# A two-layer trunk on one core: the squares' rows of x, the first unit's eviction and the rotary tables moved to other slots

## The chip, the cores and the metric

The kernel runs on one core of a Trainium2 chip. The metric is the device time of one execution in microseconds (us), taken as the median of several runs. A profiled execution is recorded besides; its trace has a start and an end for each instruction, and its times are counted from the first instruction. "PE" is the matrix engine (TensorE), "ACT" the ScalarE, "DVE" the VectorE, "POOL" the GpSimd engine; SP is the queue that issues most loads.

## The reference

Two layers of one mixer, on 256 rows of 2048 values (float32). Cut to what matters here:

```python
def hybrid_layer(x, cos, sin, norm_g, w_in, conv_w, conv_b, ...):
    h = rmsnorm(x, norm_g)
    proj = h @ w_in                                    # 2048 x 13376
    (c_a, c_glu, c_gate, q_down, kv_down, k_pe, m_gate, g_conv, g_mla) = jnp.split(proj, idx, axis=-1)
    y_conv = conv_branch(c_a, c_glu, c_gate, conv_w, conv_b, ...) @ w_proj_conv
    y_mla = mla_branch(q_down, kv_down, k_pe, m_gate, cos, sin, ...) @ w_proj_mla
    y = jax.nn.sigmoid(g_conv) * y_conv + jax.nn.sigmoid(g_mla) * y_mla
    return x + y @ w_out

def conv_branch(a, glu, gate, conv_w, conv_b, ln_g, ln_b):
    u = a * jax.nn.sigmoid(glu)
    u = (causal depthwise convolution of u, 31 taps) + conv_b
    u = jax.nn.silu(layernorm(u, ln_g, ln_b))          # over the 2048 channels
    return u * jax.nn.silu(gate)

def rope_tables(positions, dtype):
    inv_freq = ROPE_THETA ** (-jnp.arange(0, QK_ROPE, 2, dtype=jnp.float32) / QK_ROPE)
    ang = positions.astype(jnp.float32)[..., None] * inv_freq
    return jnp.cos(ang), jnp.sin(ang)
```

`rmsnorm` divides each row of x by the root of the mean of its squares. The kernel multiplies `x * norm_g` with the weights at once and applies that factor (`rinv_x`) to the products, so that it is not needed before the first products are taken out of PSUM.

## The kernel before

**Pieces.** Every product runs over the weights in pieces of 256 rows (two blocks of 128) by 320, 384 or 512 columns, one DMA each, numbered here in the order of their use: 0 to 31 are the first block of units (`glu` 0, which is 512 wide, and the three `down` blocks of 384, 384 and 320, their first two pieces interleaved), 276 is the first piece of the convolution's projection `pconv` in the first layer. A piece is split into a rounded part `hi` and a remainder `lo`: ACT casts `hi` (`split_hi`), DVE subtracts (`split_lo`), and PE multiplies high by high, low by high and high by low, 12 matmuls a piece, eight with `hi` and then four with `lo`. The activations x * g are split in the same way, on the way in, for pieces 0, 4 and 8 to 13 (`first_h`, from `x_in`).

**Buffers.** There are five buffers of raw pieces, four of `hi` and three of `lo`. So the load of a piece waits until the piece five before it is split, the cast of `hi` until PE is through with the `hi` of four before, and `lo` until PE is through with the piece three before. Splits are issued three (`HI_AHEAD`) and two (`LO_AHEAD`) pieces ahead of PE's.

**Order.** `InOrder` keeps every engine in the order of the program text that issues: what stands in an engine's queue waits for all that stands ahead of it. After each piece, `background` advances the slot clock by one (slot k follows piece k - 1) and issues what is due: `at_slot(ahead, f, ...)` puts a function on a later slot, with the cost in us that it takes of the budgets of DVE and ACT. Whatever budget is left to DVE in a slot is spent on `fill`, a first-in-first-out list that holds the convolutions (31 taps for each of eight units), and behind them the layer norm: sums over channels (`mu`, `var`, two small matmuls each), its root, the scaled and gated channels `v_t`, and at last the split `ycT` of the convolution branch, which is what `pconv` multiplies. `before_pconv` runs what is left of that list when a piece of `pconv` needs it; so the place of `ycT` in ACT's order follows from how far `fill` has come.

**The start.** In the first layer the squares of x come from eight tiles `xres` (four pairs of 128 x 512, loaded by `first_sums(t, c)`'s `begin` on SP, squared on ACT by its `end` into `ss_x`). `sum_x` adds them on DVE (`totx`) and takes the root in thirteen small instructions (`rinv_x`). Behind it come the evictions: `glu_evac` (a sigmoid on ACT, a product `su` on DVE, then the turn through DRAM that brings channels to partitions and starts the first convolution) and `down_evac` (a scaled copy). The rotary tables are made by `rope_tables`, a generator whose twelve reductions and four last steps are 3 or 4 small DVE instructions each, one step to a slot.

The lines that order this, before:

```python
at_slot(8 + a + (2 if a < 2 else 7), lambda: next(tables, None), 0.0 if a < 2 else 0.95)   # a in range(20)
...
at = 7                                                         # eviction of the first glu unit
for n, (t, c) in enumerate([(0, 0), (0, 2), (1, 0), (1, 2)]):
    begin, end = first_sums(t, c)
    at_slot((11, 12, 13, 17)[n], begin)
    at_slot((15, 16, 17, 20)[n], end, 0.0, 1.5)
at_slot(20, sum_x, 2.2)
```

Of the kernel before, what the change touches and what calls it, by code (L numbers as in the profile page):

```python
# [11 lines left out]
F32 = mybir.dt.float32  # L12
# [7 lines left out]
P = 128  # L20
T = 2
# [9 lines left out]
HALF = ROPE // 2  # L31
# [53 lines left out]
def revolution_pieces():  # L85

    from fractions import Fraction

    pi = Fraction(
        "3.14159265358979323846264338327950288419716939937510582097494459230781640628620899"  # L90
    )
    rest, out = 1 / (2 * pi), []
    for i in range(REVOLUTION_PIECES):
        unit = Fraction(1, 1 << (12 * (i + 1)))
        n = int(rest / unit)
        out.append(float(n * unit))
        rest -= n * unit
    return out
# [33 lines left out]
def trunk(ctx: ExitStack, tc: tile.TileContext, xT, x, g_in, pos, win, wuq, wukv, wpc, wpm, wo, cst, rows, invf, out):  # L132
# [19 lines left out]
    pe, vec, act, gps, sp = (InOrder(e) for e in (nc.tensor, nc.vector, nc.scalar, nc.gpsimd, nc.sync))  # L152
# [7 lines left out]
    work = pool("work", 1)  # L160
    work2 = pool("work2", 2)
# [147 lines left out]
    def at_slot(ahead, f, vec=0.0, act=0.0, first=False):  # L309
        steps.insert(0 if first else len(steps), (clock[0] + ahead, (vec, act), f))  # L310
# [280 lines left out]
    def rope_tables():  # L591

        invf_t = const.tile([P, HALF], F32, name="invf_t")
        sp.dma_start(invf_t, invf.partition_broadcast(P))
        pos_t = const.tile([P, T], I32, name="pos_t")
        sp.dma_start(pos_t, pos)
        yield
        yield
        posf = const.tile([P, T], F32, name="posf")
        vec.tensor_copy(posf, pos_t)  # L600
        tables = work.tile([P, 6, T, HALF], F32, tag="pr", name="tables")
        ang, ah, al, turn, whole, frac = (tables[:, i] for i in range(6))
        ah = ah.bitcast(F32R)
        for t in range(T):
            vec.tensor_scalar(ang[:, t, :], invf_t, posf[:, t : t + 1], None, op0=ALU.mult)
        vec.tensor_copy(ah, ang)
        vec.tensor_sub(al, ang, ah.bitcast(F32))
        yield
        big_half = 1.5 * 2.0**23

        def reduce_to(dst, src, scale):

            vec.tensor_scalar(whole, src, scale, big_half, op0=ALU.mult, op1=ALU.add)
            vec.tensor_scalar(whole, whole, -big_half, None, op0=ALU.add)
            vec.scalar_tensor_tensor(dst, src, scale, whole, op0=ALU.mult, op1=ALU.subtract)

        first = True
        for piece in revolution_pieces():
            for a in (ah.bitcast(F32), al):
                reduce_to(turn if first else frac, a, piece)  # L620
                if not first:
                    vec.tensor_add(turn, turn, frac)
                first = False
                yield
        for dst, shift in ((sin2, 0.0), (cos2, 0.25)):
            vec.tensor_scalar(frac, turn, shift, None, op0=ALU.add)
            reduce_to(ang, frac, 1.0)
            for h in range(2):
                act.activation(dst[:, :, h, :], ang, AF.Sin, scale=2.0 * np.pi)
            yield  # L630
            yield
# [24 lines left out]
    def first_sums(t, c):  # L656

        xts = []

        def begin():  # L660
            for a in (c, c + 1):
                xts.append(wide_p.tile([P, 512], F32, tag="w", name="xres"))
                sp.dma_start(xts[-1], x[t, :, a * 512 : (a + 1) * 512])

        def end():
            for a, xt in zip((c, c + 1), xts):
                junk = work.tile([P, 512], F32, tag="junk", name="junk")
                act.activation(junk, xt, AF.Square, accum_out=ss_x[:, t, a : a + 1])

        return begin, end  # L670


    for l in range(DEPTH):
# [776 lines left out]

        def rope_table_steps():
            tables = rope_tables()
            for a in range(20):
                at_slot(8 + a + (2 if a < 2 else 7), lambda: next(tables, None), 0.0 if a < 2 else 0.95)

        uses_h = stat_of(h_hi, h_lo)
        of_down = lambda k0: lambda k, t: tuple(qkc[:, i, k0 + k, t * P : (t + 1) * P] for i in range(2))
        for kind, i, pl in planned:
            if kind == "glu":
                at = 0 if i in (2, 5) else EVAC_AT  # L1460
                if i == 0 and l == 0:
                    at = 7
                    for n, (t, c) in enumerate([(0, 0), (0, 2), (1, 0), (1, 2)]):
                        begin, end = first_sums(t, c)
                        at_slot((11, 12, 13, 17)[n], begin)
                        at_slot((15, 16, 17, 20)[n], end, 0.0, 1.5)
                    at_slot(20, sum_x, 2.2)
                elif i == 0:
                    at_slot(8, sum_x, 2.2)
                if i == 0:  # L1470
                    for slot, load_const in zip(((22, 26), (4, 7))[l], load_consts):
                        at_slot(slot, load_const)
                if i == 0:
                    if l == 0:
                        rope_table_steps()
                    downs = FIRST_DOWNS[l]
                    products_together(
                        pl, uses_h, lambda i, t, ps: down_evac(i - 1, t, ps) if i else glu_evac(0, t, ps),
                        (at,) + downs * (EVAC_AT,), ((0.9, 2.2),) + downs * ((0.0, 1.0),),
                        homes=("acc", "acc") if l else ("s", "acc", "acc", "tp"),  # L1480
                    )
                    if downs == len(DOWN_BLOCKS):
                        down_after()
                    continue
                product(pl, uses_h, lambda t, ps, i=i: glu_evac(i, t, ps), at, (0.9, 2.2))
            elif kind == "down":
                product(pl, uses_h, lambda t, ps, i=i: down_evac(i, t, ps), costs=(0.0, 1.0))
                if i == len(DOWN_BLOCKS) - 1:
                    down_after()
            elif kind == "uq":  # L1490
                if i == 0:
                    attention_tiles()
                group, block = divmod(i, 3)
                product(pl, of_down(0), lambda t, ps, i=i: uq_evac(i, t, ps), costs=(0.0, (2.9, 2.7, 1.7)[block]))
                at_slot(EVAC_AT + 1, lambda b=GROUP * group + block: rotate_q(b), 1.3)
                if block == 2:
                    at_slot(EVAC_AT + LAST_ROTATE_AT, lambda b=GROUP * group + 3: rotate_q(b), 1.3)
                    attention(GROUP * group + 2)
            elif kind == "ukv":
                product(pl, of_down(4), lambda t, ps, i=i: ukv_evac(i, t, ps), costs=(0.36 * (i % GROUP == 2), 2.6))  # L1500
                if i % GROUP != 2:
                    attention(i)
                if i == NPAIR - 1:
                    layernorm()
            elif kind == "mgate":
                product(pl, uses_h, lambda t, ps, i=i: mgate_evac(i, t, ps), costs=(0.0, 3.5))
            elif kind == "gmla":
                product(pl, uses_h, lambda t, ps, i=i: gmla_evac(i, t, ps), costs=(0.0, 2.7))
            elif kind == "pmla":
                product(pl, stat_of(*keep["o"]), lambda t, ps, i=i: pmla_evac(i, t, ps), costs=(1.25, 0.0))  # L1510
            elif kind == "gconv":
                product(pl, uses_h, lambda t, ps, i=i: gconv_evac(i, t, ps), costs=(0.0, 3.9))
            elif kind == "cgate":
                product(pl, uses_h, lambda t, ps, i=i: cgate_evac(i, t, ps), costs=(0.0, 2.0))
            elif kind == "pconv":
                while "yc" not in keep:
                    run_fill()
                products_together(pl, stat_of(*keep["yc"]), pconv_evac, (EVAC_AT, EVAC_AT, EVAC_AT, 0), (2.4, 0.0), before_pconv, ("acc", "s", "tp", "acc"))
            elif i == 0:
                wout_begin(0)  # L1520
                wout_begin(1)
                products_together(pl, stat_of(*keep["y"]), wout_evac, (EVAC_AT, EVAC_AT), (1.25, 1.5))
            else:
                at_slot(3, lambda i=i: wout_begin(i))
                product(pl, stat_of(*keep["y"]), lambda t, ps, i=i, f=wout_evac: f(i, t, ps),
                        0 if i == 3 else EVAC_AT, (1.25, 1.5),
                        final=last_half if last_layer and i == 3 else None)
# [116 lines left out]
```

## Time and profile before

| what | value |
|---|---|
| median of 3 runs | 1791.65 us (1790.62 to 1792.54) |
| the profiled execution, its own time | 1791.25 us |
| its span, first to last instruction | 1789.5 us |
| granted clock of PE over the span | 0.999 |
| DMA traffic | 464.18 MB, mean 259 GB/s |

The page gives the busy time of each engine and the chain of work that ended last, of which PE makes 98%. Where PE is that full, its own waits say more than the chain: the view of waits names the engine and the tile that PE waited for, how long and how often; the timeline shows the rows around such a wait, with the idle time before a row and its releaser in brackets; and the windows give, for a stretch of time, the busy time of each engine and, in the third column from the right, the granted clock. A timeline row is a run of equal instructions, with its start, its length and their count.

### The profile page before, as it was taken

The numbers are of one execution on the slowest core, as the hardware profiler recorded it, in microseconds if no ns is written. First come the engines' busy times: TensorE is split into PE (matmuls) and PEld (weight loads), VectorE is DVE, ScalarE is ACT, GpSimd is POOL, SyncE is SP. The second block draws the span as 40 slices with busy tenths as digits, with TensorE's granted clock in tenths as the row PEclk, the third lists the DMA queues.
The fourth block names the chain that finished last, engine by engine and source line by source line (L and its number), as shares of the span: only waits on it lengthen the run. The fifth ranks groups of instructions, "written<-read, shape, count | busy, mean of one in ns | idle before, by whom it ended". The sixth has DMA issues, their size and how long they took to land.

```text
span 1789.5 us, 27098 instructions
## 1 busy us (share of the span) xinstructions
PE 1780.2 (99%) x8575; PEld 1573.0 (88%) x8575; DVE 1535.4 (86%) x2481; ACT 1297.3 (72%) x2404; POOL 553.7 (31%) x1015
## 2 busy tenths in 40 slices
PE   9999999999999999999999999999999999999999
PEld 8888888888888888888899888888888888888887
DVE  6799899898999998767668998988999999887674
ACT  6678888888877775745567788898888777666442
POOL 0155555542311120012420555656333111100210
PEclk9999999999999999999999999999999999999999
DMA  8788888887999996678887888888879889867785
GB/s 299 257 283 258 275 278 257 277 289 241 281 256 251 263 253 234 200 226 302 295 280 225 278 275 265 267 277 270 286 245 277 249 253 256 254 213 221 248 281 178
DMA packets 149967, 464.18 MB, mean 259 GB/s; under 512 B 24896, under 2 KB 31296, under 8 KB 149824
## 3 DMA queue, kind: packets, MB, share of 16 engines
q1 hardware_dynamic: 105568, 358.68, 61.7%
q0 software_dynamic: 43664, 103.24, 20.5%
q8 instruction: 67, 1.10, 0.3%
q14 instruction: 76, 0.62, 0.1%
q10 hardware_dynamic: 592, 0.54, 0.1%
HBM read 399.18 MB, written 44.04 MB: 248 GB/s over the span
## 4 chain that ended last, share of the span: by engine, by line
PE 98%; DMA 1%; ACT 0%; DVE 0%; issue 0%; SPq 0%; DVEq 0%; ACTq 0%
PE acc L143 95%; PE s L143 2%; PE o_ps L143 1%; DMA xres<-in_x 0%; DMA raw<-in_win 0%; ACT hi L143 0%; SPq L143 0%; ACT L143 0%; DVE rsq_t L143 0%; ACT v_t L143 0%; DVE xres L143 0%; ACT junk L143 0%; DVE lo L143 0%; DVE rinv_x L143 0%; ACT down L143 0%
## 5 line engine op out<-in xcount | busy, mean ns | idle before, releaser
L143 ACT CAST hi<-raw 128x1024 fp32r<-128x1024 f32 (+3 forms) x682 | 693.9, 1027 | 371.6 <-PE acc L143 277.8
L143 DVE TENSOR_TENSOR lo<-raw,hi 128x1024 fp32r<-128x1024 f32 (+3 forms) x682 | 811.9, 1194 | 154.9 <-PE acc L143 108.5
L143 PE MATMUL acc<-hi,hT 128*128 128x512 f32 (+2 forms) x1728 | 400.7, 372 | 0.0
L143 PEld LDWEIGHTS acc<-hi,hT 128*128 128x128 f32 x1728 | 319.7, 189 | 40.4
L143 PE MATMUL acc<-hi,h_hi 128*128 128x512 f32 (+2 forms) x864 | 251.2, 373 | 0.5 <-ACT hi L143 0.4
L143 PE MATMUL acc<-hi,h_lo 128*128 128x512 f32 (+2 forms) x864 | 250.7, 372 | 0.0
L143 DVE SCALAR_TENSOR_TENSOR v_t<-u_t,cst,v_t 128x256 f32<-128x256 f32 x556 | 237.3, 480 | 2.0
L143 PE MATMUL acc<-lo,h_hi 128*128 128x512 f32 (+2 forms) x864 | 220.5, 372 | 1.5 <-DVE lo L143 1.5
L143 PE MATMUL acc<-lo,hT 128*128 128x512 f32 (+2 forms) x864 | 220.2, 372 | 0.0
L143 PEld LDWEIGHTS acc<-lo,h_hi 128*128 128x128 f32 x864 | 160.7, 189 | 22.9 <-DVE lo L143 2.3
L143 PEld LDWEIGHTS acc<-hi,h_lo 128*128 128x128 f32 x864 | 161.5, 189 | 20.6
L143 PEld LDWEIGHTS acc<-lo,hT 128*128 128x128 f32 x864 | 160.8, 189 | 20.6
L143 PEld LDWEIGHTS acc<-hi,h_hi 128*128 128x128 f32 x864 | 160.3, 189 | 21.2 <-ACT hi L143 1.1
L143 POOL DMA_DIRECT2D turn_d<-gate x176 | 96.2, 554 | 218.7 <-DVE gate L143 157.9
L143 POOL DMA_DIRECT2D taps<-taps x73 | 64.2, 879 | 306.2 <-ACT taps L143 232.3
L143 ACT ACTIVATE taps<-u_t,cst 128x256 f32<-128x256 f32 x302 | 132.8, 498 | 0.3 <-DVE v_t L143 0.3
L143 PE MATMUL acc<-hi,ycT 128*128 128x512 f32 x512 | 124.0, 383 | 2.3 <-ACT ycT L143 2.2
L143 PE MATMUL acc<-hi,oT 128*128 128x512 f32 x512 | 122.2, 379 | 0.0
L143 PE MATMUL acc<-hi,yT 128*128 128x512 f32 x512 | 122.0, 378 | 0.0
L143 POOL DMA_DIRECT2D turned<-turn_d x88 | 50.2, 578 | 213.8 <-ACT hi L143 61.0
L143 PEld LDWEIGHTS acc<-hi,ycT 128*128 128x128 f32 x512 | 97.4, 191 | 17.0 <-ACT ycT L143 2.6
L143 PE MATMUL acc<-hi,qkc 128*128 128x512 f32 x448 | 110.4, 379 | 0.0
(181 smaller groups left out, 2356.8 us busy)
## 6 DMA issues: line engine op xcount, KB each, us to landing
raw<-in_win SPq DMA_DIRECT2D x384, 512.0 KB, 4.8
raw<-in_wpm SPq DMA_DIRECT2D x64, 512.0 KB, 4.9
raw<-in_wpc SPq DMA_DIRECT2D x64, 512.0 KB, 4.2
raw<-in_wo SPq DMA_DIRECT2D x64, 512.0 KB, 5.2
taps<-taps POOLq DMA_DIRECT2D x73, 256.0 KB, 6.1
raw<-in_wukv SPq DMA_DIRECT2D x32, 512.0 KB, 4.4
turned<-turn_d POOLq DMA_DIRECT2D x56, 256.0 KB, 5.5
raw<-in_wuq SPq DMA_DIRECT2D x24, 512.0 KB, 4.8
```

The source lines that it names most:

```text
L143: ins = getattr(self.engine, name)(*a, **k)
```

## The change

```diff
     def rope_tables():
         invf_t = const.tile([P, HALF], F32, name="invf_t")
-        sp.dma_start(invf_t, invf.partition_broadcast(P))
+        gps.dma_start(invf_t, invf.partition_broadcast(P))
         pos_t = const.tile([P, T], I32, name="pos_t")
-        sp.dma_start(pos_t, pos)
+        gps.dma_start(pos_t, pos)
...
-        tables = work.tile([P, 6, T, HALF], F32, tag="pr", name="tables")
-        ang, ah, al, turn, whole, frac = (tables[:, i] for i in range(6))
+        tables = work.tile([P, 4, T, HALF], F32, tag="sx", name="tables")
+        steps_of = work2.tile([P, 2, T, HALF], F32, tag="qr", name="table_steps", bufs=3)
+        ang, ah, al, turn = (tables[:, i] for i in range(4))
+        whole, frac = (steps_of[:, i] for i in range(2))
...
         def rope_table_steps():
             tables = rope_tables()
-            for a in range(20):
-                at_slot(8 + a + (2 if a < 2 else 7), lambda: next(tables, None), 0.0 if a < 2 else 0.95)
+            next(tables)
+            next(tables)
+            for slot in (5, 6, 7, 8, 15, 16, 17, *range(21, 32)):
+                at_slot(slot, lambda: next(tables, None), 0.95)
...
                 if i == 0 and l == 0:
-                    at = 7
+                    at = 5
                     for n, (t, c) in enumerate([(0, 0), (0, 2), (1, 0), (1, 2)]):
                         begin, end = first_sums(t, c)
-                        at_slot((11, 12, 13, 17)[n], begin)
-                        at_slot((15, 16, 17, 20)[n], end, 0.0, 1.5)
-                    at_slot(20, sum_x, 2.2)
+                        at_slot((9, 10, 11, 14)[n], begin)
+                        at_slot((13, 13, 14, 17)[n], end, 0.0, 1.5)
+                    at_slot(18, sum_x, 2.2)
```

The rows of x are asked for two slots sooner (the last pair three), squared two to three sooner, and the root is taken at slot 18 in place of 20. The first unit is evicted at slot 19 in place of 21. The two small loads for the tables go from SP, between weight loads, to POOL at the program's start. The tables no longer share a buffer with the gains, which are in use until x is split, so their steps can begin at slot 5; four come there, three at slots 15 to 17, none at 18 to 20, the rest from 21 on.

On SP's queue, before, the last pair of `xres` stands behind the load of piece 23 (a number behind `raw` is the piece's):

```order
L143 DMA xres_467<-in_x 128x512
L143 DMA xres_469<-in_x 128x512
L143 DMA raw20_475<-in_win 128x768
L143 DMA raw21_493<-in_win 128x768
L143 DMA raw22_515<-in_win 128x768
L143 DMA raw23_537<-in_win 128x768
L143 DMA xres_555<-in_x 128x512
L143 DMA xres_557<-in_x 128x512
```

and now, with the first pairs higher up too, behind that of piece 20:

```order
L143 DMA xres_450<-in_x 128x512
L143 DMA xres_452<-in_x 128x512
L143 DMA raw18_458<-in_win 128x768
L143 DMA raw19_476<-in_win 128x768
L143 DMA raw20_502<-in_win 128x768
L143 DMA xres_520<-in_x 128x512
L143 DMA xres_522<-in_x 128x512
L143 DMA raw21_528<-in_win 128x768
```

Each of the first three pairs moved past two weight loads, the fourth past three.

On DVE, before, the root (from `totx` to the last `rinv_x`; ten of its rows left out) stands behind `lo` of piece 21, and table steps stand on both sides of `lo` of piece 22:

```order
L143 TENSOR_TENSOR lo21_609<-raw21_493,hi21_589 128x768
L143 TENSOR_REDUCE totx_631<-ss_x_143 128x2
...
L143 SCALAR_TENSOR_TENSOR rinv_x_142<-rsq_t_635,rinv_x_142 128x2
L143 TENSOR_SCALAR tables_561<-tables_561 128x64 x2
L143 SCALAR_TENSOR_TENSOR tables_561<-tables_561 128x64
L143 TENSOR_TENSOR tables_561<-tables_561 128x64
L143 TENSOR_TENSOR lo22_651<-raw22_515,hi22_611 128x768
```

and now behind `lo` of piece 19, with no table step before `lo` of piece 23:

```order
L143 TENSOR_TENSOR lo19_594<-raw19_476,hi19_570 128x768
L143 TENSOR_REDUCE totx_612<-ss_x_143 128x2
...
L143 SCALAR_TENSOR_TENSOR rinv_x_142<-rsq_t_616,rinv_x_142 128x2
L143 TENSOR_TENSOR lo20_628<-raw20_502,hi20_596 128x768
L143 SCALAR_TENSOR_TENSOR su_646<-acc0_00_161,rinv_x_142,su_646 128x256
L143 SCALAR_TENSOR_TENSOR su_650<-acc0_01_162,rinv_x_142,su_650 128x256
L143 TENSOR_TENSOR lo21_664<-raw21_528,hi21_630 128x768
L143 TENSOR_TENSOR lo22_682<-raw22_550,hi22_666 128x768
```

The root moved up by two pieces, the first unit's `su` by two, and the table steps out from among them.

On ACT, much later, where `pconv` begins with piece 276, before (the number behind `v_t` tells one unit of the convolution from another):

```order
L143 CAST hi277_7766<-raw277_7678 128x1024
L143 ACTIVATE v_t_2615<-v_t_2615,cst_146 128x256 x2
L143 ACTIVATE v_t_4849<-v_t_4849,cst_146 128x256 x2
L143 CAST hi278_7788<-raw278_7703 128x1024
L143 CAST hi279_7824<-raw279_7724 128x1024
L143 ACTIVATE v_t_5479<-v_t_5479,cst_146 128x256 x2
L143 CAST ycT0_7809<-v_t_1035 128x512
L143 CAST ycT0_7809<-v_t_2615 128x512
L143 ACT_TABLE_LOAD
```

and now:

```order
L143 CAST hi276_7752<-raw276_7667 128x1024
L143 CAST hi277_7781<-raw277_7688 128x1024
L143 ACTIVATE v_t_5440<-v_t_5440,cst_146 128x256 x2
L143 CAST ycT0_7773<-v_t_970 128x512
L143 CAST ycT0_7773<-v_t_2138 128x512
L143 CAST hi278_7805<-raw278_7710 128x1024
L143 CAST hi279_7832<-raw279_7732 128x1024
L143 ACT_TABLE_LOAD
L143 ACTIVATE sc_7303<-acc268_0_7634,rinv_x_142 128x512
```

No line of the diff speaks of this place. Since the first unit is evicted sooner, its convolution enters `fill` sooner, and with the budgets that rule there the whole list has moved up by two pieces; the casts of `ycT` went past those of pieces 278 and 279.

## The prediction

> **What bounds the kernel now.** I read the page's busy shares first, then the waits of TensorE, then TensorE's rows at each wait, then the rows of the engine waited for. First the page:
>
> ```profile
> PE 1780.2 (99%) x8575; PEld 1573.0 (88%) x8575; DVE 1535.4 (86%) x2481; ACT 1297.3 (72%) x2404; POOL 553.7 (31%) x1015
> ```
>
> PE is busy 1780.2 us of a span of 1789.5 us. No reordering of other engines can bring more than the 9.3 us in which PE idles, and what PE loses while it is busy but slow. The waits of PE say where it idles:
>
> ```profile
> PE acc L143 <- ACT ycT L143: 2.2, 1, 2.2
> PE acc L143 <- DVE lo L143: 1.5, 2, 0.8
> ```
>
> Both are places in the first layer; what PE idles beside them is at its start and after its end. The timeline of PE at the place of the `lo` waits (each piece of weights is five rows: four of `hi`, one of `lo`; the first row of a piece is `hi,h_hi`):
>
> ```profile
> 51.18 0.49 PE L143 MATMUL acc<-hi,h_hi 128*128 128x384 f32 x2
> ...
> 53.13 0.49 PE L143 MATMUL acc<-hi,h_hi 128*128 128x384 f32 x2
> ...
> 56.12 0.49 PE L143 MATMUL acc<-hi,h_hi 128*128 128x384 f32 x2
> ...
> 59.03 0.49 PE L143 MATMUL acc<-hi,h_hi 128*128 128x384 f32 x2
> ```
>
> These are pieces 21 (51.18), 22 (53.13), 23 (56.12) and 24 (59.03). An undisturbed piece takes 53.13 - 51.18 = 1.95 us. Pieces 22 and 23 take 5.90 us from 53.13 to 59.03, where two take 3.90: **2.00 us are lost here**. A piece wants its `lo` after 8 of its 12 matmuls, 1.30 us after its start: piece 20 (started 49.23, 1.95 before 51.18) at 50.53, piece 21 at 52.48, piece 22 at 54.43.
>
> Why `lo` is late, in the rows of the SP queue, of ACT and of DVE:
>
> ```profile
> 37.15 5.85 SPq L143 DMA_DIRECT2D raw<-in_win  x4
> 43.05 0.90 SPq L143 DMA_DIRECT2D xres<-in_x  x2
> ```
> ```profile
> 49.53 0.63 ACT L143 ACTIVATE junk<-xres 128x512 f32<-128x512 f32 x1 [0.78 <-DMA xres<-in_x]
> ```
> ```profile
> 51.04 0.16 DVE L143 TENSOR_REDUCE totx<-ss_x 128x2 f32<-128x8 f32 x1 [2.30 <-ACT junk L143]
> ...
> 53.50 0.42 DVE L143 TENSOR_SCALAR tables<-tables 128x64 f32<-128x64 f32 x2
> ...
> 54.36 0.95 DVE L143 TENSOR_TENSOR lo<-raw,hi 128x768 fp32r<-128x768 f32 x1
> ...
> 56.48 0.88 DVE L143 SCALAR_TENSOR_TENSOR su<-acc,rinv_x,su 128x256 f32<-128x256 f32 x2 [0.32 <-ACT su L143]
> 57.27 0.95 DVE L143 TENSOR_TENSOR lo<-raw,hi 128x768 fp32r<-128x768 f32 x1
> ```
>
> The last pair of `xres` tiles is issued at 43.05 behind four weight loads and lands 6.5 us later, at 49.53. ACT squares it, DVE waits 2.30 us in its queue for the sum, and behind the root and one table step stands `lo` of piece 22 (54.36); behind another table step and the two `su` stands `lo` of piece 23 (57.27).
>
> The second place, the start of the convolution's projection (piece 276), again PE, then ACT:
>
> ```profile
> 728.17 0.59 PE L143 MATMUL acc<-lo,h_hi 128*128 128x512 f32 x2
> 731.02 3.65 PE L143 MATMUL acc<-hi,ycT 128*128 128x512 f32 x8 [2.25 <-ACT ycT L143]
> ...
> 735.59 1.89 PE L143 MATMUL acc<-hi,ycT 128*128 128x512 f32 x8
> ...
> 738.18 1.89 PE L143 MATMUL acc<-hi,ycT 128*128 128x512 f32 x8
> ```
> ```profile
> 723.53 1.03 ACT L143 CAST hi<-raw 128x1024 fp32r<-128x1024 f32 x1
> ...
> 728.42 1.05 ACT L143 CAST hi<-raw 128x1024 fp32r<-128x1024 f32 x1 [0.94 <-ACT hi L143]
> 729.37 1.09 ACT L143 ACTIVATE v_t<-v_t,cst 128x256 f32<-128x256 f32 x2
> 730.36 1.12 ACT L143 CAST ycT<-v_t 128x512 fp32r<-128x512 f32 x2
> 731.50 1.28 ACT L143 ACT_TABLE_LOAD   x1
> 732.80 1.27 ACT L143 ACTIVATE sc<-acc,rinv_x 128x512 f32<-128x512 f32 x2
> ```
>
> A piece of 512 columns takes 738.18 - 735.59 = 2.59 us, 0.216 a matmul. The two matmuls of the row at 728.17 would let piece 276 start at 728.60 and piece 277 at 731.19; it starts at 735.59. **4.40 us are lost here**, of which only 731.02 - 728.60 = 2.42 are waiting. The other 1.98 is PE at half speed; a window of 1 us shows the granted clock (0.50, the figure ahead of the last two):
>
> ```profile
> 732.00:733.00 1.00, 1.00 (x3) 0.82 (x4) 0.29 (x1) 0.99 (x2) 0.00 (x0) 0.50 0.72 184
> ```
>
> The wait itself: the cast of `ycT` stands in ACT's queue behind the cast of piece 279 (728.42), whose buffer, one of four, is that of piece 275, the last that PE multiplies before. So `ycT` cannot come before PE has run dry.
>
> The Trainium skill ("TensorE: Matmul & The Clock Gate", "What's actually happening") puts the fall to half clock behind an idle window of about 3.4 us. By that rule a gap of 2.42 us would cost nothing more, this place would be worth 2.42, and the sum below would come to 1787.2. The row above shows clock 0.50 behind the shorter gap, so for this execution the measurement decides.
>
> **The change part by part.**
>
> *Rows of x.* The four pairs are asked for at slots 9, 10, 11, 14 in place of 11, 12, 13, 17. The last pair before was the one at 43.05, slot 17; slot 14 is in the middle of the weight loads that begin at 37.15, so I take 37.5, and with the same 6.5 us it lands at 44.0 in place of 49.53. The two squarings that this pair needs last 1.5 us (49.53 to 51.04). The root (from 51.04 to the table step at 53.50, some 2.5 us) now stands right behind `lo` of piece 19, whose buffer, one of three, PE frees with piece 16 at 43.38 (51.18 - 4 x 1.95), so that this `lo` ends near 44.4. The root runs from 45.5 to 48.0. Then `lo` 20 ends at 49.0 (wanted 50.53: 1.5 to spare), the two `su` at 49.9 (the table load ahead of their sigmoid, 1.28 us, no longer follows `down` but runs while ACT waits for the root), `lo` 21 at 50.8 (wanted 52.48: 1.7 to spare), `lo` 22 at 51.8 (wanted 54.43). **Minus 2.00.** Bounds: the spare is used up if the pair lands 1.5 us later than I take; a landing after 49.53 would cost more than before.
>
> *Table steps.* A step is some 0.9 us (53.50 to 54.36), and none now stands between `lo` 19 and `lo` 22. Their number is the same. Four go to slots 5 to 8, where DVE is not the bound:
>
> ```profile
> 24.32 0.91 ACT L143 ACTIVATE h_hi<-x_in,gx 128x256 fp32r<-128x256 f32 x2 [1.34 <-DMA x_in<-in_xT]
> 25.13 1.03 ACT L143 CAST hi<-raw 128x1024 fp32r<-128x1024 f32 x1
> ```
> ```profile
> 27.17 0.59 PE L143 MATMUL acc<-hi,h_hi 128*128 128x512 f32 x2
> ```
>
> Here ACT waits for `x_in`, and piece 10 is split at 26.16 for PE at 27.17: 1.0 us to spare, the tightest of the pieces there. Four steps are some 3.5 us; each falls mostly into a wait of DVE for ACT. What is left delays a `lo` by up to half a us, and through the freed buffer the next load of SP. Between 0 and 3.5 - 1.0 = 2.5 us of PE; I take 0, since the waits for `x_in` come once per piece and the steps do too.
>
> *Two small loads from SP to POOL; other tags for the tables.* POOL has nothing else to issue before the first `su`, and `sx` and `qr` are not needed again before attention. I take 0. The two loads, 17 KB, now run beside the first weights, so PE could start later; as the end of the range I take 0.6, a tenth of the 6.5 us that a pair of `xres` thirty times their size takes to land.
>
> *First unit two slots sooner.* The convolution is a queue of steps taken as DVE's budget allows, so everything behind moves up: mean and variance stand two pieces sooner in PE's order, and at piece 276 the cast of `ycT` now stands behind `hi` 277, not 279. That cast's buffer is that of piece 273 and was free before 723.53. The last that `ycT` needs of DVE is this row, two pieces or 5.18 us sooner:
>
> ```profile
> 728.02 1.43 DVE L143 TENSOR_TENSOR v_t<-turned,v_t 128x256 f32<-128x256 f32 x4
> ```
>
> DVE is through at 729.45 - 5.18 = 724.3; ACT, with `hi` 277 at 724.6, `v_t` 1.09 and `ycT` 1.12, at 726.8 or before. PE wants it at 728.60: 1.8 to spare. No wait, so no half clock: **minus 4.40.** Late next would be `hi` 280: from 728.3 ACT now has `hi` 279 (1.05), a table load, two `sc` (1.3), a table load, four `v_t` (2.1) and `hi` 280 (1.05), in all 8.1 us, to 736.4; PE wants it at 728.60 + 4 x 2.59 = 738.96. Six fewer tap products on ACT and six more on DVE fall where PE does not wait at all; I take 0.
>
> *Sum.* The profiled run took 1791.25 us (span 1789.5 and 1.75 around it): 1791.25 - 2.00 - 4.40 = 1784.85. The median of the runs is 0.40 higher, so 1785.25; I give **1785.2**, 0.36% faster. No-change, about what a measurement can tell, is 0.2% or 3.6 us.
>
> **The rivals.**
>
> *The second place stays* (12%). Another operand of piece 276, or `hi` 280, is late, PE waits over 2 us there and the clock falls again. For it: three engines meet there and my spare is 1.8. Against: the order frees `ycT` from the end of the block. Only 2.00 is gained: 1789.6.
>
> *The change does not do what it says* (8%): the rows of x are asked for sooner but land no sooner, since `x_in` and weights fill the DMA engines. The root then ends at 53.5 as before, but now `lo` 20 waits behind it, ready at 54.5 and wanted at 50.53: 4.0 us of waiting and 2.0 at half clock, as at the second place. 1791.65 - 4.40 - 2.00 + 6.0 = 1791.2. Against it: an earlier load does not wait behind later ones in a queue.
>
> *A part of it* (8%): `lo` 20 or 21 still late by 1 to 2.5 us, 1786.2 to 1787.7; or the timed runs of before did not have the half clock that the profiled one had, so that only 2.42 can go at the second place: 1791.65 - 2.00 - 2.42 = 1787.2. For the latter: the three runs spread by 1.9 us, which is the size of that loss.
>
> *Slower* (4%): four squarings (3 us) now stand in ACT's queue ahead of `hi` 16, which PE wants at 49.23 - 4 x 1.95 = 41.43. If the first two pairs land at X, `hi` 16 is ready at X + 3.0 + 0.8, so PE waits from X = 37.6 on; the first pair is now issued behind the last `x_in`, the second one piece later:
>
> ```profile
> 27.82 0.43 SPq L143 DMA_DIRECT2D x_in<-in_xT  x1
> ```
>
> That is 28.3 and 30.9, and 6.5 later is 37.4. Every us more is one of PE, and a wait over 2 us costs 2.0 more by the clock. From X = 42 on the gain is gone; at X = 46 the time is 1791.65 - 6.4 + 8.4 + 2.0 = 1795.7. Against it: that is twice the time to landing of any such load before.
>
> **How the numbers follow.** Forecast 68%, its own range 1783.6 to 1786.2 (the runs before spread by that much and the small terms add to it). Faster by over 0.2% is under 1788.1: forecast and part, 0.76; same: the second place and the loads that land no sooner, 0.20; slower 0.04. The range must leave out no more than 2 in 10: with the part and the second place, up to 1789.6, it holds some 0.85 (a little of the forecast lies outside).
>
> **What would show it.** PE waits neither for `lo` nor for `ycT`; the windows behind 726 us show clock 1.00; the last `xres` pair is issued near 37.5 and squared before 46; the `totx` row follows `lo` of piece 19 with under 1.5 us of idle. The forecast is wrong if PE waits for `hi` between 25 and 43 us, or for `lo` at pieces 20 and 21, or shows clock 0.50 anywhere after its start.

## The result, and the profile after

The change makes the kernel faster by 0.24%: the ratio of the mean times is 0.9976, with a 95% interval of 0.9969 to 0.9984. The medians are 1786.33 us (16 runs) and, before, 1791.38 us (16 runs), 5.05 us apart. Ratios below are made in the same way, each against runs of the kernel before that were taken beside it. The profiled run took 1786.36 us. In it PE is busy for all but 6.7 us of the span. The page's first lines, of after:

```profile
span 1784.6 us, 27089 instructions
...
PE 1777.9 (100%) x8575; PEld 1575.3 (88%) x8575; DVE 1538.4 (86%) x2487; ACT 1295.4 (73%) x2398; POOL 551.7 (31%) x1014
```

The waits of PE, of after (engine and tiles waited for, then us in total, how often, the longest):

```profile
PE acc L143 <- ACT hi L143: 1.3, 2, 0.8
PE warm L143 <- PEq L1637: 0.8, 1, 0.8
```

The waits for `lo` and for `ycT` are gone. For `hi` there are two, both in pieces 0 and 1, where before had one of 0.4 us, ahead of piece 2. The first place, the timeline of PE, of after, first rows of pieces 21 to 24:

```profile
52.85 0.49 PE L143 MATMUL acc<-hi,h_hi 128*128 128x384 f32 x2
...
54.80 0.49 PE L143 MATMUL acc<-hi,h_hi 128*128 128x384 f32 x2
...
56.75 0.49 PE L143 MATMUL acc<-hi,h_hi 128*128 128x384 f32 x2
...
58.70 0.49 PE L143 MATMUL acc<-hi,h_hi 128*128 128x384 f32 x2
```

Pieces 22 and 23 take 58.70 - 54.80 = 3.90 us, where before they took 5.90. What stands behind it, in the rows of SP, of ACT and of DVE, of after:

```profile
39.32 1.16 SPq L143 DMA_DIRECT2D xres<-in_x  x2
```
```profile
47.03 0.63 ACT L143 ACTIVATE junk<-xres 128x512 f32<-128x512 f32 x1 [1.25 <-DMA xres<-in_x]
```
```profile
47.79 0.16 DVE L143 TENSOR_REDUCE totx<-ss_x 128x2 f32<-128x8 f32 x1 [0.55 <-ACT junk L143]
...
50.27 0.96 DVE L143 TENSOR_TENSOR lo<-raw,hi 128x768 fp32r<-128x768 f32 x1
51.14 0.87 DVE L143 SCALAR_TENSOR_TENSOR su<-acc,rinv_x,su 128x256 f32<-128x256 f32 x2
51.93 1.82 DVE L143 TENSOR_TENSOR lo<-raw,hi 128x768 fp32r<-128x768 f32 x2
```

The last pair of `xres` is issued at 39.32; its first tile lands at 45.0 (ACT squares it at 45.06) and its second at 47.0. DVE waits 0.55 us for the sum, where it waited 2.30. `lo` of piece 20 (50.27) is done at 51.23 and wanted at 52.20, so 0.97 us is left.

The second place, PE and then ACT, of after:

```profile
727.57 0.59 PE L143 MATMUL acc<-lo,h_hi 128*128 128x512 f32 x2
728.00 1.89 PE L143 MATMUL acc<-hi,ycT 128*128 128x512 f32 x8
...
730.60 1.89 PE L143 MATMUL acc<-hi,ycT 128*128 128x512 f32 x8
```
```profile
722.21 1.06 ACT L143 CAST hi<-raw 128x1024 fp32r<-128x1024 f32 x1 [0.51 <-ACT hi L143]
723.17 1.09 ACT L143 ACTIVATE v_t<-v_t,cst 128x256 f32<-128x256 f32 x2
724.16 1.12 ACT L143 CAST ycT<-v_t 128x512 fp32r<-128x512 f32 x2
725.19 1.04 ACT L143 CAST hi<-raw 128x1024 fp32r<-128x1024 f32 x1
```

`ycT` is cast behind `hi` of piece 277 (722.21) and is done 2.7 us before PE wants it. Piece 276 follows without a gap and takes 2.59 us, from 728.00 to 730.60: all of the 4.40 us is gone. (A piece's length is the difference of the starts of two first rows, taken before they are rounded, so that it can differ by 0.01 us from the rows shown.)

These two make 6.40 us; the profiled run is 4.89 faster. What was given back is at the start. ACT's casts of the first pieces, of before and then of after:

```profile
5.50 0.44 ACT L143 CAST hi<-raw 128x320 fp32r<-128x320 f32 x1
6.31 0.51 ACT L143 CAST hi<-raw 128x384 fp32r<-128x384 f32 x1 [0.36 <-DMA raw<-in_win]
8.13 1.82 ACT L143 CAST hi<-raw 128x1024 fp32r<-128x1024 f32 x2 [1.31 <-DMA raw<-in_win]
```
```profile
6.86 0.46 ACT L143 CAST hi<-raw 128x320 fp32r<-128x320 f32 x1 [1.34 <-DMA raw<-in_win]
...
8.18 0.51 ACT L143 CAST hi<-raw 128x384 fp32r<-128x384 f32 x1 [0.87 <-DMA raw<-in_win]
...
9.47 1.82 ACT L143 CAST hi<-raw 128x1024 fp32r<-128x1024 f32 x2 [0.77 <-DMA raw<-in_win]
```

The same casts stand 1.3 to 1.9 us later, each behind its weights' DMA. PE starts piece 2 at 10.56 us in place of 9.23: **1.33 us lost**. (Counted from PE's first product, which came 0.25 us sooner, at 4.56 in place of 4.81, it is 1.58; the expectations below take 1.6.) The page's windows of 1 us, of before and then of after, end with the DMA engines' share and the GB/s:

```profile
4.00:5.00 1.00, 0.90 (x5) 0.67 (x5) 0.96 (x3) 0.46 (x2) 0.00 (x0) 1.00 1.18 313
5.00:6.00 1.00, 1.00 (x7) 0.84 (x7) 0.90 (x3) 0.94 (x3) 0.00 (x0) 1.00 0.95 360
```
```profile
4.00:5.00 1.00, 0.90 (x6) 0.56 (x5) 0.96 (x3) 0.61 (x2) 0.00 (x0) 1.00 1.30 158
5.00:6.00 1.00, 0.91 (x6) 0.84 (x6) 1.00 (x3) 0.51 (x2) 0.00 (x0) 1.00 0.66 96
```

From 4 to 6 us the DMA engines move 158 and 96 GB/s where they moved 313 and 360. That is when the two small loads are under way, which POOL now issues at the start (the DMA issues in the first 9 us, of after: KB, and us from issue to landing):

```profile
invf_t<-in_invf POOLq DMA_DIRECT2D x1, 16.0 KB, 5.1
pos_t<-in_pos POOLq DMA_DIRECT2D x1, 1.0 KB, 5.0
```

The rest is small: pieces 11 and 12 took 0.33 us more (PE waits for `hi` of piece 12, behind the last `x_in`), piece 76 took 0.07 more, pieces 31 and 33 took 0.34 less. With -6.40 and +1.33 that makes -5.01 of the -4.89.

### The profile page after: what moved, and what is told of

It reads as the page before. It is cut to its first block, busy times and chain, and to the rows that moved or that the text cites. A ratio compares the mean times of both kernels' runs of the same rounds, so it can differ in the third digit from the quotient of the medians.

```text
span 1784.6 us, 27089 instructions
## 1 busy us (share of the span) xinstructions
PE 1777.9 (100%) x8575; PEld 1575.3 (88%) x8575; DVE 1538.4 (86%) x2487; ACT 1295.4 (73%) x2398; POOL 551.7 (31%) x1014
## 4 chain that ended last, share of the span: by engine, by line
PE 98%; DMA 1%; DVE 0%; ACT 0%; SPq 0%; issue 0%; DVEq 0%
PE acc L143 95%; PE s L143 2%; PE o_ps L143 1%; DMA x_in<-in_xT 1%; DMA raw<-in_win 0%; DVE lo L143 0%; SPq L143 0%; ACT hi L143 0%; DVE xres L143 0%; ACT h_hi L143 0%; DVE h_lo L143 0%; DVE table_steps L143 0%; PE var L143 0%; PE mu L143 0%; DVE tables L143 0%
## 5 line engine op out<-in xcount | busy, mean ns | idle before, releaser
L143 ACT ACTIVATE taps<-u_t,cst 128x256 f32<-128x256 f32 x292 | 128.4, 498 | 0.4 <-DMA taps<-taps 0.4
L143 PEld LDWEIGHTS acc<-hi,oT 128*128 128x128 f32 x512 | 97.0, 190 | 13.5
```

What stands on the lines that cost most here:

```text
L143: ins = getattr(self.engine, name)(*a, **k)
```

## The experiments

Three theories stood after this reading. **Steps**: the convolution's list moved up because the table steps end at slot 31 and no longer at 34; each takes 0.95 us of DVE's budget, and the line `budget[e] = min(budget[e], 0.0) + slot - split_us` lets no unused budget pass from one slot to the next, so a step at slots 5 to 8 takes nothing from the list and one at 34 does. **Unit**: the list moved up because the first unit is evicted sooner, as the prediction has it. **Small loads**: they cost the start its 1.33 us; against it stood scatter of the first loads. The runs below compute all that the reference asks for.

**Small loads late.** Both on SP in place of POOL, behind the first weights.

```
-        gps.dma_start(invf_t, ...)
+        sp.dma_start(invf_t, ...)
-        gps.dma_start(pos_t, pos)
+        sp.dma_start(pos_t, pos)
...
-            next(tables)
-            next(tables)
+            for slot in (2, 3):
+                at_slot(slot, lambda: next(tables, None), 0.0)
```

> The changed kernel, with the two small loads (invf_t, pos_t) back in SP's queue, at slots 2 and 3, in place of POOL's at the start; all else as changed. Theory A: these two loads beside the first weights cost the start of the program 1.6 us (piece 2 starts at 10.56 us in the changed kernel, at 9.23 before), so piece 2 starts near 9.2 again and the time is 1786.3 - 1.6 = 1784.7. Rival: the late start is scatter of the first loads from one execution to the next; then the time stays at 1786.3 and piece 2 may start anywhere.

Measured: 1785.63 us, 0.9968 of before (0.9956 to 0.9981); piece 2 starts at 9.44 us. Once more, on another chip:

> The changed kernel with the small loads on SP at slots 2 and 3, once more, beside the two below on one chip: 1785.6 as in its first runs, or 1786.5 if those were a lucky set.

Measured: 1786.61 us, 0.9974 (0.9964 to 0.9985); piece 2 at 8.98. The windows of 1 us, of the first of these:

```profile
4.00:5.00 1.00, 0.90 (x5) 0.63 (x5) 0.96 (x4) 0.66 (x3) 0.00 (x0) 1.00 1.08 352
5.00:6.00 1.00, 1.00 (x8) 1.00 (x9) 1.00 (x4) 0.68 (x2) 0.00 (x0) 1.00 0.94 356
```

The bandwidth is back (352, 356 GB/s) and so is the start, but the time is hardly below that of the changed kernel. In both profiles PE then loses time that the changed kernel's first profile does not: at piece 75, 0.50 and 0.75 us, waiting for `qk_t` of DVE; in the first 0.14 at pieces 9 and 10; in the second, where it comes sooner still, at pieces 20 (0.66), 30 (0.28), 50 (0.25) and 195 (0.28). PE at piece 75, of the second run:

```profile
188.34 0.67 PE L143 MATMUL acc<-hi,h_hi 128*128 128x512 f32 x2 [0.59 <-DVE qk_t L143]
```

So the start is shown; that its 1.3 us come out at the end is not.

**The small loads alone.** The kernel before, with `sp` made `gps` in the two loads and both issued at the start; steps at slots 17 to 34.

> The kernel before, with only the two small loads moved to POOL at the start of the program; the table steps stay at slots 17 to 34. Theory A: only the start gets longer, pieces 0 and 1 by 1.6 us together, and the time is 1791.4 + 1.6 = 1793.0. Rival: scatter, 1791.4, piece 2 starts at 9.2 as before.

Measured: 1792.37 us, 1.0005 (0.9996 to 1.0014), and piece 2 at 10.57 us. The time alone does not tell the two apart; the start does.

**The small loads by ACT.** The changed kernel with `act.dma_start` for the two, still at the start.

> The changed kernel with the two small loads at the start of the program, but issued by ACT in place of POOL, so that they go by a hardware queue. Each costs ACT 0.45 us ahead of its first cast, which had waited 0.56, so PE starts some 0.35 later. Theory A1 (POOL's software queue delays the first weights, the bytes don't): piece 2 starts near 9.6 and the time is 1785.3. Theory A2 (any two loads in many small packets beside the first weights delay them): piece 2 starts at 10.6 or later, 1786.3 to 1786.7.

Measured: 1787.02 us, 0.998 (0.9971 to 0.9988), piece 2 at 9.92 us. The windows of 1 us:

```profile
4.00:5.00 1.00, 0.90 (x6) 0.73 (x5) 0.96 (x3) 0.56 (x2) 0.00 (x0) 1.00 1.03 287
5.00:6.00 1.00, 1.00 (x7) 0.84 (x7) 1.00 (x3) 0.69 (x3) 0.00 (x0) 1.00 0.87 192
```

The dip is there (287, 192 GB/s), but it is shallower than with POOL's queue. The start lies between the two theories, and this one profile does not settle how much is the queue and how much the packets.

**The changed kernel again**, on one chip with the small loads by ACT and two runs further below.

> The changed kernel once more, beside the three below on one chip. If its start is as in its first profile, piece 2 starts near 10.6 us and the time is 1786.3; if that start was scatter, piece 2 starts anywhere from 8.9 to 10.6.

Measured: 1786.58 us, 0.9976 (0.9967 to 0.9985); piece 2 at 10.64 us. Over all profiles but that with the loads by ACT, piece 2 starts at 10.56, 10.57, 10.64 and 10.02 where POOL issues the small loads at the start, and from 8.50 to 9.55 in the nine where SP issues them later. The two sets do not overlap, and their means are 10.45 and 9.12. Pieces 11 and 12 lose nothing in this profile, so their 0.33 us was scatter. Instead it loses 1.04 us at piece 195, waiting for `lo`:

```profile
PE acc L143 <- DVE lo L143: 0.8, 1, 0.8
```

DVE there stands idle for 3.47 us ahead of a row that takes `taps`, which comes by DMA, and `lo` of piece 195 follows that row. The same place cost 1.09 us in the profile with the small loads by ACT (3.37 us of idle) and nothing in the changed kernel's first profile (2.99 us). So PE loses time at places that differ from one profile of the same kernel to the next, and an earlier start can be lost there again.

**The steps alone.** The changed kernel, small loads late, with rows and unit as before:

```
-                    at = 5
+                    at = 7
...
-                        at_slot((9, 10, 11, 14)[n], begin)
-                        at_slot((13, 13, 14, 17)[n], end, 0.0, 1.5)
-                    at_slot(18, sum_x, 2.2)
+                        at_slot((11, 12, 13, 17)[n], begin)
+                        at_slot((15, 16, 17, 20)[n], end, 0.0, 1.5)
+                    at_slot(20, sum_x, 2.2)
```

> The changed kernel without its rows of x (loads again at slots 11, 12, 13, 17, squares and root behind them) and with the first unit evicted at 7 again; the small loads on SP at slots 2 and 3. What is left of the change is the table steps at slots 5 to 8, 15 to 17 and 21 to 31. Theory A (the table steps, which now end three slots sooner, are what moves the convolution up by two pieces): the 4.4 us at pieces 275 and 276 are gone, clock 1.00 there; at the first place lo of piece 22 comes about in time, but piece 23 still waits some 1.8 us behind su; so 1791.4 - 4.4 - 0.2 = 1786.8. Rival B (as predicted, the unit evicted two slots sooner moves it): PE waits for ycT by 2.2 us again with clock 0.50 behind it, time 1791.2. Rival C (the table steps alone cure both places): 1785.0.

Measured: 1788.34 us, 0.9981 (0.9972 to 0.999). In ACT's order `ycT` stands behind `hi` of piece 277, and PE goes through the second place without a wait:

```profile
729.36 0.59 PE L143 MATMUL acc<-lo,h_hi 128*128 128x512 f32 x2
729.80 1.89 PE L143 MATMUL acc<-hi,ycT 128*128 128x512 f32 x8
```

At the first place `lo` of piece 23 stands behind `su`, and the loss there is 1.95 us as before (DVE, then PE):

```profile
57.53 0.88 DVE L143 SCALAR_TENSOR_TENSOR su<-acc,rinv_x,su 128x256 f32<-128x256 f32 x2 [1.16 <-ACT su L143]
58.32 0.95 DVE L143 TENSOR_TENSOR lo<-raw,hi 128x768 fp32r<-128x768 f32 x1
```
```profile
59.33 0.92 PE L143 MATMUL acc<-lo,h_hi 128*128 128x384 f32 x4 [1.54 <-DVE lo L143]
```

Theory Steps is borne out for the second place, Unit falls. The time is 1.5 above what was expected: pieces 8 to 10 lose 0.81 and piece 75 0.15.

**The rows and the unit alone.** The kernel before with those four lines as changed, and the tables as before.

> The kernel before with the rows of x, the root and the first unit as changed, and the tables wholly as before (loads on SP at slots 10 and 11, steps at slots 17 to 34). Theory A: the wait for ycT stays, 2.2 us and 4.4 us lost with the half clock; the first place loses less than its 2.0 us, but table steps of 0.9 us each stand again between lo of pieces 19 to 22, so that 0 to 1.1 us of it stay: 1789.4 to 1790.5. Rival B (the unit sooner moves the convolution up): pieces 275 and 276 take 2.59 us each, time 1785.0 to 1786.1.

Measured: 1790.49 us, 0.9995 (0.9987 to 1.0004): no gain that can be told. The wait for `ycT` is as before. At the first place PE now waits at pieces 20 and 21, which take 3.24 and 2.50 us, 1.84 too much; in DVE's rows a table step (49.73, 50.19) stands between the root, whose last row is at 49.66, and `lo` of piece 20 (50.33), another and `su` before that of piece 21. That is more than the 1.1 expected. Pieces 30, 31, 48, 50 and 75 lose another 2.58 us in this profile, where before lost 0.24 (at piece 31); their cause stays open. The waits of PE, then DVE:

```profile
PE acc L143 <- ACT ycT L143: 2.3, 1, 2.3
PE acc L143 <- DVE lo L143: 1.3, 2, 1.0
```
```profile
49.73 0.42 DVE L143 TENSOR_SCALAR tables<-tables 128x64 f32<-128x64 f32 x2
50.19 0.22 DVE L143 SCALAR_TENSOR_TENSOR tables<-tables 128x64 f32<-128x64 f32 x1
50.33 0.95 DVE L143 TENSOR_TENSOR lo<-raw,hi 128x768 fp32r<-128x768 f32 x1
```

So neither the rows nor the steps cure the first place alone: the rows make the root early, and the steps must also make way.

**The unit at 7.** The changed kernel with `at = 7` in place of 5.

> The changed kernel with the first unit evicted at 7, as before, all else as changed. Theory A (the table steps that end three slots sooner moved the convolution up; the unit's two slots do nothing there): pieces 275 and 276 take 2.59 us, the time is that of the changed kernel, 1786.3, within 0.5. Rival B (as predicted, the unit moved it): 4.4 us are lost there again, 1790.7.

Measured: 1786.84 us, 0.998 (0.9971 to 0.9989); pieces 275 and 276 take 2.59 us. The time is that of the changed kernel, so the unit's two slots do nothing that can be measured.

**How far the steps must move.** The kernel with the small loads late, and only the last eleven steps moved: `range(25, 36)`, then `range(28, 39)`, in place of `range(21, 32)`.

> The kernel of the run above with its last eleven table steps at slots 25 to 35 in place of 21 to 31, and nothing else. In ACT's order the first cast of ycT then stands behind hi of piece 278 (behind 277 in the changed kernel, 279 before). By the rows of before, v_t and the first half of ycT then end near 729.03 where PE wants it at 728.60: PE waits some 0.5 us, too short for the half clock, and the time is 0.5 over that of the run above. Rival (the steps' place has no part in it): no difference.

Measured: 1784.93 us, 0.9968 (0.9956 to 0.998), with no wait for `ycT`. The expected half us did not come, because `hi` of piece 278 is cast at 722.73, 3.7 us sooner than before, while PE wants `ycT` only 2.7 us sooner (at 725.94 for 728.60); `ycT` starts at 724.68. PE's only wait:

```profile
PE warm L143 <- PEq L1637: 0.8, 1, 0.8
```

The steps end one slot later here than before the change, at 35, and yet `ycT` stands one piece sooner, behind 278: the last slot alone does not set the place. Before, three steps also stood at slots 18 to 20, and a cost above the budget is carried on; how much each counts was not tried.

> As the run above, with the last eleven table steps at slots 28 to 38: ycT then stands behind hi of piece 279, as before the change, while the rows of x and the first unit are as changed. Theory A: PE waits 2.25 us for ycT, the start of the convolution's projection loses 2.8 without and 4.4 with the half clock behind it, and the time is 2.8 to 4.4 over that of the first run of this call, 1788.4 to 1790.0; whether the half clock comes differs from one execution to the next. Rival B (the unit sooner cured that place): no difference.

Measured: 1792.7 us, 1.0005 (0.9996 to 1.0014), so all of the gain is lost. PE, then the windows of 1 us (the granted clock is the third figure from the end):

```profile
727.07 0.59 PE L143 MATMUL acc<-lo,h_hi 128*128 128x512 f32 x2
730.65 3.42 PE L143 MATMUL acc<-hi,ycT 128*128 128x512 f32 x8 [2.99 <-ACT ycT L143]
...
735.32 1.89 PE L143 MATMUL acc<-hi,ycT 128*128 128x512 f32 x8
```
```profile
732.00:733.00 1.00, 1.00 (x3) 0.74 (x3) 0.00 (x0) 0.99 (x2) 0.00 (x0) 0.50 0.74 250
```

The wait is 2.99 us and the two pieces take 10.42 for 5.18, a loss of 5.24. The median is 6.1 above the 1786.61 of the small loads late, taken beside it, where 2.8 to 4.4 were expected; the profiled run, at 1790.94, is one of this kernel's faster ones, and what the slower ones lose beyond it was not seen.

**The faster version, again.**

> The kernel with ycT behind hi of piece 278 once more, for its time against before: 1784.9 as in its first runs (0.9968 of before), with no wait for ycT and pieces 275 and 276 at 2.59 us each; or 1786.3, that of the changed kernel, if its first six runs were a lucky set.

Measured: 1785.4 us, 0.9966 (0.9954 to 0.9979). In both sets this version, with the small loads late and the last steps at slots 25 to 35, is 0.9 to 1.7 us below the changed kernel's 1786.33 and 1786.58; the intervals of the ratios still overlap.

**The four early steps elsewhere.** The changed kernel with the small loads on SP at slot 5 and the steps of slots 5 to 8 at 11 to 14.

> The changed kernel with the small loads on SP at slot 5 and the four steps of slots 5 to 8 at slots 11 to 14, where PE had 1.9 us to spare before: meant to be faster than both. If the start and the pieces 8 to 12 then lose nothing, the profile's sum is 1786.36 - 1.6 (start) - 0.33 (pieces 11 and 12) = 1784.4. If the four steps delay lo of pieces 13 to 16 or the root instead, PE waits for lo there and the time stays above 1785.4.

Measured: 1786.09 us, 0.9976 (0.9966 to 0.9986). The gain expected, to 1784.4, did not come. Piece 2 starts 1.0 us sooner than in the changed kernel, but the last `xres` is issued only 0.3 sooner, at 39.03, and `lo` of piece 20 comes just too late: that piece takes 2.24 us for 1.95. The larger loss is at piece 195 again: 1.29 us, with DVE idle for 3.30 us ahead of the row that takes `taps`. The last pair of rows stands in SP's queue behind weight loads whose buffers DVE frees with its `lo`, and at 11 to 14 the steps come ahead of those `lo`; that this is the cause at piece 20 was read from the queues and not tried.

## Why the prediction was right in the time, and where it was wrong

The measured 1786.33 us lies 0.13 above the forecast's own range (1783.6 to 1786.2) and well inside the wide one, up to 1789.6. By its number it is in the interval of the rival "a part of it", but not by that rival's cause: no `lo` was late. That the second place was cured although its cause was named wrongly is in part luck: the prediction read the place of `ycT` from the order of the whole changed kernel, which holds the effect of every edit, so the size did not depend on which edit made it.

- **Rows of x, minus 2.00**: right. Pieces 22 and 23 lost 2.00 us less. Its times were early: the last pair was issued at 39.32 and not at 37.5, landed at 45.0 and 47.0 and not at 44.0, and the spare for `lo` of pieces 20 and 21 was 0.97 and 1.27 us for the predicted 1.5 and 1.7. 1.33 us of the later times is the late start, which moves PE as well. That the steps between those `lo` must go too, which the prediction says in a sentence on the table steps, is half of the cure: the rows without them left 1.84 us of loss there.
- **First unit two slots sooner, minus 4.40**: the size is right for this pair of profiles, the cause is wrong, and with it the sentence ahead of the prediction that the list moved up since the unit is evicted sooner. The order of before and of after showed that it had moved, not which edit moved it. With the unit at 7 again nothing changed; with the unit at 5 and the steps at 17 to 34 the wait stayed. It was the table steps, a part that the prediction priced at nothing: moving the last eleven of them, and nothing else, put `ycT` behind `hi` of piece 277, 278 or 279. How their slots lead to that place, by the unused budget, is argued from the code and was not traced. What stood behind the move held: `ycT` had time to spare, and `hi` of piece 280, named as late next, was done at 735.72 and wanted at 738.37.
- **Two small loads, taken at 0 with 0.6 as the end of the range**: the term that was mis-sized. They cost the start 1.33 us, in this pair of profiles and in the means over all. The price was scaled from the landing time of a load thirty times larger; with these 17 KB under way, the DMA rate of the first weights fell to 158 and 96 GB/s. This is most of the 1.5 us between the predicted sum (1784.85) and the profiled run (1786.36).
- **Table steps at slots 5 to 8, taken at 0**: as delay, at most the 0.33 us of pieces 11 and 12, which the next profile of the same kernel does not have.
- **What would show it**: no wait for `lo` or `ycT`, clock 1.00 behind 726 (it falls to 0.68 and 0.50 only from 1782 on, when PE's last product is done) and 0.55 us of idle ahead of `totx` came as written. The last pair's issue near 37.5 and its square before 46 did not. PE did wait for `hi` between 25 and 43 us, by 0.33, which the prediction named as a sign of being wrong; the mechanism held all the same, and the next profile of the same kernel does not show that wait.
- **The half clock**: the 4.40 held 1.98 us of it, and it does not come behind every such gap. Two other kernels with the same gap of 2.25 us (the small loads alone; the rows and the unit alone) show piece 276 at 2.99 us and clock 1.00 behind the gap, so that the place cost them 2.81. So the place was worth between 2.81 and 4.40, and the timed gain of 5.05 us is a difference of medians over executions of both kinds, as the last section suggests; the prediction's remark that the timed runs of before might lack the half clock then holds for some of them.

## What to carry to other kernels

Where an order is made from budgets, find by building it with one edit at a time which edit moves a distant place; the difference of two orders shows only that all of them did. Work that has slack belongs in slots where nothing else could use the engine, since a slot's unused budget is lost. Loads that nobody needs yet stay out of the first microseconds, however small they are; here that brought the start forward by 1.3 us, though not all of it reached the end.

## What the runs showed of the hardware

Two loads of 17 KB together, issued by POOL beside the first weights, lowered the DMA rate from 313 and 360 GB/s to 158 and 96 for two microseconds, and landed only after 5 us themselves; by ACT's queue it was 287 and 192. Over all profiles the rates in these two windows are 81 to 158 and 85 to 111 GB/s in the four with POOL, and 277 to 352 and 330 to 389 in the nine where SP issues the loads later.

The half clock does not follow every short gap of PE. The windows of 1 us behind the 2.25 us gap of the kernel with the small loads alone:

```profile
732.00:733.00 1.00, 0.47 (x2) 0.30 (x2) 0.58 (x2) 1.00 (x2) 0.00 (x0) 1.00 0.95 242
733.00:734.00 1.00, 0.97 (x5) 0.68 (x4) 0.81 (x2) 0.98 (x2) 0.00 (x0) 1.00 0.88 315
```

The clock is 1.00 here, where before, behind a gap of the same 2.25 us, it was 0.50. Behind a gap of 1.54 us, at the first place of the steps alone, it was 1.00 too.

These are different kernels with one profile each. That one kernel differs between its executions is what the timed runs suggest: 86 runs of the kernel before were taken beside the experiments, each with its mean granted clock. It is 1.000 in 36 of them, with a median of 1789.90 us, and 0.998 or 0.999 in 50, with a median of 1791.84: 1.94 us apart, close to the 1.98 of the half clock. That mean also counts the end of the program, where PE is done, so this agrees with the half clock in some executions and does not prove it.

The Trainium skill ("TensorE: Matmul & The Clock Gate", "What's actually happening") says that PE's activity is judged in windows of some 3.4 us that run freely, so that the point at which a starting kernel's clock changes depends on where in a window its first matmul falls. The half clock behind one gap out of three of the same length agrees with windows that run freely. That a full idle window of about 3.4 us is needed, as the same section of the Trainium skill has it, does not agree with the traces, since gaps of 2.25 and 2.99 us had the half clock.
